# Part of a block-wise matrix product done in seven products of quarters instead of eight

## The chip, the cores and the metric

The kernel runs on one core of one Trainium2 chip. The metric is the device time of one execution in microseconds (us). The core's engines work side by side, each through its own queue in order: TensorE (PE in the rows, its weight loads PEld), VectorE (DVE), ScalarE (ACT), GpSimd (POOL) and SyncE (SP), which here issues the loads. What a matmul writes lands in PSUM; the rest lives in SBUF.

## The reference

A decoder trunk of two layers over 256 tokens of 1024 channels. Each layer has a mixer (attention in the first, a convolution module in the second) and an expert mixer with 16384 experts, and this last one takes most of the time:

```python
def peer(h, w_pq, sub_keys, expert_u, expert_v):
    ...
    def chunk(args):
        xc, ec, gc = args
        u = expert_u[ec]
        act = jax.nn.gelu(jnp.einsum('cd,chkd->chk', xc, u))
        w = gc.astype(xc.dtype) * act
        return jnp.einsum('chk,chkd->cd', w, expert_v[ec])
```

The kernel doesn't gather the 128 chosen experts of each token. It multiplies all experts: the first table gives a value for every expert and token, the gates (zero where an expert isn't chosen) are multiplied in, and the second table is multiplied with the result: out[256 tokens, 1024] = W[256, 16384] x V[16384, 1024]. The change is in this second product.

## The kernel before, in words

Everything is fp32. A product is made from parts: each operand is rounded to a high part (`hi`, written by ScalarE) and the rest is kept as a low part (`lo`, written by VectorE), and `mm3` (lines 126 to 132) does three matmuls: high by high, high by low, low by high. Each streams 512 columns.

The second table comes in 128 blocks of 128 experts, two at a time: 64 pairs in each layer (line 612). For a pair, the 512 weights per expert row (two blocks of 256 tokens) lie in the store tile `st`; ScalarE writes their high parts `wh` (line 616) and VectorE their low parts `wo` (line 617), in a ring of four pairs. Then `s2` (line 159) takes the two blocks of the table by `weights` (line 98): SP loads a block of 128x1024 into one of four `raw` buffers (line 95), ScalarE casts it to one of three `hi` buffers (line 106), VectorE subtracts to one of three `lo` buffers (line 112). The sums of the whole stage lie in four PSUM banks `acc[t][h]`, t one of two tiles of 128 tokens, h one of two halves of 512 channels. A pair is thus eight products (two blocks, two t, two h) of three matmuls: 24.

At the end of a layer's stage the four banks are added to the residual `x` (line 221) when the next norm is made. In the first layer, from the middle of the stage on, ScalarE also writes scaled diagonals for the convolution that follows (line 423), three a pair.

The order in which each engine's instructions go out is not that of the code: a planner of the language (`schedule_with_timeline_sim=True`) orders them, by the order of the code and by when it thinks operands and buffers are ready. Only where `after` or `keep_in_program_order` stands is the order given by hand.

Of the kernel before, what the change touches and what calls it, by code (L numbers as in the profile page):

```python
# [7 lines left out]
F32 = mybir.dt.float32  # L8
F32R = mybir.dt.float32r
# [3 lines left out]
ALU = mybir.AluOpType  # L13
AX = mybir.AxisListType

P = 128
D = 1024
KC = D // P
T = 256
# [13 lines left out]
NK = 128  # L33
# [4 lines left out]
HI = NK // 2  # L38
# [3 lines left out]
G0 = 24  # L42
G1 = 60
OH = 3 * NK * TB
TMP = 512 + NT * D


# [9 lines left out]
class Trunk:  # L57
# [101 lines left out]
    def s2(self, acc, src, aTs, n0, n, pool_share=0, between=None):  # L159

        if n0 + len(aTs) == n:
            pool_share = 0
        blocks = [(n0 + k, self.weights(src[n0 + k], pool_share), a) for k, a in enumerate(aTs)]
        th = [(t, h) for t in range(NT) for h in range(2)]
        if n0 + len(aTs) == n:
            order = [(b, t, h) for t, h in th for b in blocks]  # L170
        elif n0 == 0:
            order = [(b, t, h) for t in range(NT) for b in blocks for h in range(2)]
        else:
            order = [(b, t, h) for b in blocks for t, h in th]
        prev = None
        for (i, w, a), t, h in order:
            if n0 == 0 and t == 1 and between is not None:
                between()
                between = None
            mms = self.s2_mm(acc, w, a, t, h, i == 0, i == n - 1)  # L180
            if n0 + len(aTs) == n:
                if prev is not None:
                    self.after(mms[0], prev)
                prev = mms[-1]


    def setup(self):
# [59 lines left out]
    def norm_open(self, g):  # L247
        self.xT = [self.one.tile([P, KC, T], F32R, tag=k, name=self.nm(k)) for k in ("xh", "xo")]
        self.g = g
        self.tmp = self.cutter(self.work.tile([P, TMP], F32, tag="oh", name=self.nm("tmp")))  # L250
        self.junk = self.tmp(512)
# [316 lines left out]
    def peer(self, l, acc):  # L568
        nc, I = self.nc, self.I
        new = lambda: self.store_tile("st").rearrange("p (i t) -> p i t", t=T)  # L570
        st = [new()]
        sl = lambda i: st[i // HI][:, i % HI:i % HI + 2, :]

        g = self.gain(2 * l + 1, st[0][:, HI - D // T:, :].rearrange("p i t -> p (i t)"))
        xT = self.norm_T(g, acc)
        U, V = I["u"][l], I["v"][l]
        self.route_open(l)
        for h in range(PH):
            ps = self.s1_pair([I["wpq"][l, 2 * h], I["wpq"][l, 2 * h + 1]], xT, POOL_Q, h == 0)
            qT = self.qT[h % 2]  # L580
            nc.scalar.copy(qT, ps)
            self.route_scores(l, h, qT)
        route = self.route_steps()
        steps = 2 * (PH + 13)
        nb = T // TB
        half = NK // 4
        done = 0
        for pi in range(NK // 2):
            if pi == G0:
                for _ in route:  # L590
                    pass
                st.append(new())
                self.gates_open()
                self.one_hots(0)
            due = min(max(0, pi + 1 - G0) * nb // (G1 - G0), nb)
            todo = list(range(done, due))
            done = due
            ps = self.s1_pair([U[2 * pi], U[2 * pi + 1]], xT,
                              between=lambda j: [self.gate_bank(b, j, 2 * pi, st) for b in todo])
            for b in todo:  # L600
                if b + 1 < nb:
                    self.one_hots(b + 1)
            self.expert_rows(ps, sl(2 * pi), done * TB)
            if pi < G0:
                for _ in range((pi + 1) * steps // G0 - pi * steps // G0):
                    next(route, None)
        acc = self.s2_open()
        ring = 4
        wh = self.one.tile([P, ring, 2, T], F32R, tag="xh", name=self.nm("wh"))
        wo = self.one.tile([P, ring, 2, T], F32R, tag="xo", name=self.nm("wo"))  # L610
        w0 = self.work.tile([P, 2, 2, T], F32R, tag="oh", name=self.nm("w0"))
        for pi in range(NK // 2):
            w, r = sl(2 * pi), pi % ring

            h, o = (wh[:, r], wo[:, r]) if pi else (w0[:, 0], w0[:, 1])
            nc.scalar.copy(h, w)  # L616
            nc.vector.tensor_tensor(o, w, h.bitcast(F32), op=ALU.subtract)  # L617
            parts = [(h[:, j, :], o[:, j, :]) for j in range(2)]
            self.s2(acc, V, parts, 2 * pi, NK)
            if pi < half:  # L620
                pass
            elif l + 1 == DEPTH:
                if pi == half:
                    self.g_out = self.gain(2 * DEPTH, self.store_tile("g")[:, 0:D])
            else:
                if pi == half:
                    prep = self.conv_prep(l + 1)
                for _ in range(-(-(CDG + 1) // half)):
                    next(prep, None)
        return acc  # L630
# [130 lines left out]
    def gates_open(self):  # L761
        oh = self.work.tile([P, 2 * OH], F16, tag="oh", name=self.nm("oh"))
        self.oh = oh.rearrange("p (r k t n e) -> p r k t n e", r=2, k=3, t=TB // 2, e=2)
# [53 lines left out]
    def finish(self, acc):  # L817
        nc = self.nc
        tmp = self.cutter(self.work.tile([P, TMP], F32, tag="oh", name=self.nm("tmp")))
        junk = tmp(512)  # L820
# [90 lines left out]
```

## Time and profile before

| | |
|---|---|
| median of 3 runs | 1880.69 us (1880.18 to 1880.77) |
| the profiled execution's own time | 1880.45 us |
| its span, first to last instruction | 1878.5 us |
| busy: TensorE, VectorE, ScalarE | 1848.9, 1308.0, 943.4 us |
| mean granted TensorE clock | 0.996 |

The profile is of one execution. Its span is 1.95 us shorter than that execution's time, for what lies before the first and after the last instruction. A matmul's row gives its duration from start to end; as matmuls overlap, 389 ns for one of 512 columns is not what it costs in a stream, which is the distance from start to start. The stage that is changed runs from about 590 to 931 us in the first layer and from about 1527 to 1871 us in the second.

### The profile page before, as it was taken

To read this page: it belongs to the slowest core of one execution; us is meant where nothing else is said; L and a number is where in the kernel's file an instruction comes from. 1 tells how busy PE (TensorE), PEld (TensorE's weight loads), DVE (VectorE), ACT (ScalarE), POOL (GpSimd) and SP (SyncE) were. 2 spreads that over 40 slices of the span, in tenths; PEclk is the share of its full clock that TensorE was granted. 3 is DMA by queue.
4 is the path that set the end of the run, shared out by engine and by line. 5 is a ranking of instruction groups with operands and counts; after the bars stand their busy time and mean duration, and the time that the engine had idled before them with its cause. 6 is when DMAs were issued, how large, how long until landed. Compare 5 with 4: busy or idle time off the path is not lost. (4 is left out here: it accounts for less than half of the span.)

```text
span 1878.5 us, 32197 instructions
## 1 busy us (share of the span) xinstructions
PE 1848.9 (98%) x12668; PEld 1690.4 (90%) x12668; DVE 1308.0 (70%) x2501; ACT 943.4 (50%) x1429; POOL 146.3 (8%) x107
## 2 busy tenths in 40 slices
PE   8999999999999999999999899999999999999998
PEld 6979999999999888888798799999999998888886
DVE  4669984788895555555587599748888855555555
ACT  4753455554445444666463534555544444444443
POOL 1213000000000000000075430000000000000000
PEclk9999999999999999999999999999999999999999
DMA  7345555444445555555542455554444455555553
GB/s 266 139 138 177 180 186 185 158 157 158 158 158 185 194 193 206 193 198 191 180 147 68 131 180 174 190 181 152 163 158 157 158 189 192 193 206 196 190 192 133
DMA packets 91736, 326.32 MB, mean 174 GB/s; under 512 B 10176, under 2 KB 12480, under 8 KB 91584
## 3 DMA queue, kind: packets, MB, share of 16 engines
q1 hardware_dynamic: 91584, 324.26, 50.5%
q8 instruction: 99, 1.62, 0.4%
q14 instruction: 53, 0.43, 0.1%
HBM read 323.17 MB, written 1.05 MB: 173 GB/s over the span
## 5 line engine op out<-in xcount | busy, mean ns | idle before, releaser
L106 ACT CAST hi<-raw 128x1024 fp32r<-128x1024 f32 x600 | 628.7, 1049 | 635.8 <-PE ps_h L146 409.4
L112 DVE TENSOR_TENSOR lo<-raw,hi 128x1024 fp32r<-128x1024 f32 x554 | 677.3, 1223 | 330.9 <-ACT hi L106 329.9
L146 PE MATMUL ps_h<-xh,hi 128*128 128x256 f32 x2560 | 734.9, 288 | 0.0
L146 PE MATMUL ps_h<-xh,lo 128*128 128x256 f32 x2560 | 721.5, 283 | 0.0
L146 PE MATMUL ps_h<-xo,hi 128*128 128x256 f32 x2560 | 718.2, 283 | 0.0
L146 PEld LDWEIGHTS ps_h<-xh,hi 128*128 128x128 f32 x2560 | 490.4, 192 | 2.0 <-issue 1.0
L146 PEld LDWEIGHTS ps_h<-xh,lo 128*128 128x128 f32 x2560 | 490.0, 192 | 0.0
L146 PEld LDWEIGHTS ps_h<-xo,hi 128*128 128x128 f32 x2560 | 488.0, 192 | 0.2
L131 PE MATMUL acc<-lo,wh 128*128 128x512 f32 x1008 | 391.1, 389 | 0.0
L132 PE MATMUL acc<-hi,wo 128*128 128x512 f32 x1008 | 391.1, 389 | 0.0
L130 PE MATMUL acc<-hi,wh 128*128 128x512 f32 x1008 | 271.3, 389 | 0.0
L132 PEld LDWEIGHTS acc<-hi,wo 128*128 128x128 f32 x1008 | 189.2, 188 | 39.4
L130 PEld LDWEIGHTS acc<-hi,wh 128*128 128x128 f32 x1008 | 189.2, 188 | 39.3
L131 PEld LDWEIGHTS acc<-lo,wh 128*128 128x128 f32 x1008 | 189.2, 188 | 39.2
L617 DVE TENSOR_TENSOR wo<-st,wh 128x512 fp32r<-128x512 f32 x126 | 86.7, 691 | 98.8 <-ACT wh L616 98.8
L616 ACT CAST wh<-st 128x512 fp32r<-128x512 f32 x126 | 77.9, 623 | 148.8 <-PE acc L131 148.8
L112 POOL TENSOR_TENSOR lo<-raw,hi 128x1024 fp32r<-128x1024 f32 x46 | 109.6, 2390 | 136.2 <-ACT hi L106 116.7
L228 POOL TENSOR_TENSOR sums<-sums,mhalf 128x1 f32<-128x1 f32 x10 | 8.7, 872 | 1009.3 <-DVE sums L225 1009.3
L793 PE MATMUL ps_g<-oh 128*128 128x128 f16 x1024 | 81.5, 220 | 0.0
L801 DVE SCALAR_TENSOR_TENSOR st<-ps_g,st 128x256 f32<-128x256 f32 (+4 forms) x224 | 74.5, 351 | 8.5 <-PE ps_g L793 8.5
L781 DVE TENSOR_TENSOR oh<-iota,slot 128x1024 f16<-128x1024 f16 x64 | 44.3, 692 | 47.8 <-PE ps_g L793 47.8
L804 ACT ACTIVATE st<-ps_g 128x256 f32<-128x256 f32 (+19 forms) x156 | 42.2, 289 | 69.1 <-DVE st L801 69.1
(168 smaller groups left out, 1242.3 us busy)
## 6 DMA issues: line engine op xcount, KB each, us to landing
raw<-in_u_dram SPq DMA_DIRECT2D x256, 512.0 KB, 3.3
raw<-in_v_dram SPq DMA_DIRECT2D x256, 512.0 KB, 3.3
raw<-in_wpq_dram SPq DMA_DIRECT2D x32, 512.0 KB, 3.4
raw<-in_pw_dram SPq DMA_DIRECT2D x24, 512.0 KB, 3.3
raw<-in_wqk_dram SPq DMA_DIRECT2D x16, 512.0 KB, 3.4
raw<-in_wv_dram SPq DMA_DIRECT2D x8, 512.0 KB, 6.3
raw<-in_wo_dram SPq DMA_DIRECT2D x8, 512.0 KB, 3.2
att<-in_bias_dram SPq DMA_DIRECT2D x4, 512.0 KB, 8.9
```

The lines of the kernel that those rows point to most:

```text
L106: ins = [nc.scalar.copy(hi, raw)]
L112: ins.append(eng.tensor_tensor(lo, raw, hi.bitcast(F32), op=ALU.subtract))
L130: return [mm(ps, wh, xh, start=first, stop=False), mm(ps, wh, xo, start=False, stop=False), mm(ps, wo, xh, start=False, stop=last)]
L131: mm(ps, wh, xo, start=False, stop=False),
L132: mm(ps, wo, xh, start=False, stop=last)]
L146: self.nc.tensor.matmul(ps[:, j, :], w[:, c * P:(c + 1) * P], x[:, c, :], start=n == 0, stop=n == len(terms) - 1)
L616: nc.scalar.copy(h, w)
L617: nc.vector.tensor_tensor(o, w, h.bitcast(F32), op=ALU.subtract)
L781: nc.vector.tensor_tensor(g0, iota, slot(0), op=ALU.is_equal)
L793: nc.tensor.matmul(ps[:, t, :], self.oh[:, b % 2, 0, tp, :, e], self.oh[:, b % 2, 1 + k, tp, :, e], start=k == 0, stop=k == 1)
L801: nc.vector.scalar_tensor_tensor(v, ps[:, :, lo:lo + m].rearrange("p t i -> p i t"), 1.0 / GS, v, op0=ALU.mult, op1=ALU.mult)
L804: nc.scalar.activation(st[half][:, m:HI, ts], ps[:, :, lo + m:lo + HI].rearrange("p t i -> p i t"), AF.Copy, scale=1.0 / GS)
```

## The change

17 of the 64 pairs of a layer (`FAST`, three or four pairs apart) go another way, `s2_seven`. The pair's product is seen as a product of two by two quarters (weights: two token tiles by two blocks of 128x128; table: two blocks by two halves of 128x512), and Strassen's scheme in Winograd's form does it in seven products instead of eight. For that VectorE makes four sums or differences of weight quarters (three of them written over the weights of the pair before, one in place) and four of table quarters (`mix`). ScalarE and VectorE then split into high and low parts seven weight quarters at once and seven table quarters in four pieces, which take four of the ring's `hi` and `lo` buffers instead of two. Three of the seven products go straight into banks of `acc`; the other four are gathered over all 17 pairs in four more PSUM banks (`quarters`), which stand in the pools of the stages before. After pair 60, `seven_end` adds these four to `x` by one copy and eight additions. The ring of `wh` and `wo` is cut from four pairs to two, and the seven weight quarters take the room behind it.

```diff
+FAST = (3, 6, 10, 13, 17, 20, 24, 27, 30, 34, 38, 41, 45, 48, 52, 55, 59)
...
+    def s2_seven(self, acc, q, srcs, a, at, parts, first, last):
...
+        nc = self.nc
+        sub = lambda o, x, y: nc.vector.tensor_tensor(o, x, y, op=ALU.subtract)
+        s1, s2, s4, a11, a21, a12, a22 = (a[:, at + k * P:at + (k + 1) * P] for k in range(-3, 4))
+        nc.vector.tensor_tensor(s1, a21, a22, op=ALU.add)
+        sub(s2, s1, a11)
+        sub(s4, a12, s2)
+        sub(a21, a11, a21)
+        ah, ao = parts
+        seven = a[:, at - 3 * P:at + 4 * P]
+        nc.scalar.copy(ah, seven)
+        sub(ao, seven, ah.bitcast(F32))
+        A = {k: (ah[:, n * P:(n + 1) * P], ao[:, n * P:(n + 1) * P])
+             for n, k in enumerate(("s1", "s2", "s4", "11", "s3", "12", "22"))}
+        left, right = slice(0, 512), slice(512, D)
+        t1, t3, t2, t4 = (self.mix[:, k, :] for k in range(4))
+        r1, r2 = (self.load(s) for s in srcs)
+        sub(t1, r1[:, right], r1[:, left])
+        sub(t3, r2[:, right], r1[:, right])
+        sub(t2, r2[:, right], t1)
+        sub(t4, r2[:, left], t2)
+        B = {}
+        for v, names in ((r1[:, left], ("11",)), (r2, ("21", "22")),
+                         (self.mix[:, 0:2, :].rearrange("p k n -> p (k n)"), ("t1", "t3")),
+                         (self.mix[:, 2:4, :].rearrange("p k n -> p (k n)"), ("t2", "t4"))):
+            n = 512 * len(names)
+            hi, lo = (self.whl.tile([P, D], F32R, tag=k, name=self.nm(k))[:, 0:n] for k in ("hi", "lo"))
+            nc.scalar.copy(hi, v)
+            sub(lo, v, hi.bitcast(F32))
...
+        for to, x, y in ((q[1], "11", "11"), (acc[0][0], "12", "21"), (acc[0][1], "s4", "22"),
+                         (q[5], "s1", "t1"), (q[7], "s3", "t3"), (q[6], "s2", "t2"), (acc[1][0], "22", "t4")):
+            mine = any(to is v for v in q.values())
+            self.mm3(to, A[x], B[y], first and mine, last and mine)
+
+    def seven_end(self, q):
...
+        nc.scalar.copy(one, q[1])
+        add(u, q[6], one)
+        add(x(0, 0), x(0, 0), one)
+        add(x(0, 1), x(0, 1), u)
+        add(x(0, 1), q[5], x(0, 1))
+        add(u, q[7], u)
+        add(x(1, 0), x(1, 0), u)
+        add(x(1, 1), x(1, 1), u)
+        add(x(1, 1), q[5], x(1, 1))
...
-        ring = 4
...
+            if pi in FAST:
+                fast = slice(4 * T, 4 * T + 7 * P)
...
+                self.s2_seven(acc, quarters, (V[2 * pi], V[2 * pi + 1]), flat, at, (wh[:, fast], wo[:, fast]),
+                              pi == FAST[0], pi == FAST[-1])
+            else:
+                n = 2 * T
+                r = pi % 2 * n
...
+            if pi == FAST[-1] + 1:
+                self.seven_end(quarters)
```

## Rows read from the trace of the kernel before

**Rows 1.** The page: busy time of each engine and its share, and two lines of the span in 40 slices (TensorE's busy tenths and its granted clock in tenths).
```profile
PE 1848.9 (98%) x12668; PEld 1690.4 (90%) x12668; DVE 1308.0 (70%) x2501; ACT 943.4 (50%) x1429; POOL 146.3 (8%) x107
...
PE   8999999999999999999999899999999999999998
...
PEclk9999999999999999999999999999999999999999
```

**Rows 2.** The page: the chain that ended last, shares of the span by line.
```profile
PE ps_h L146 22%; PE acc L130 6%; PE acc L132 6%; PE acc L131 6%; PE ps_g L793 2%; PE ps_s L676 0%; PE ps_t L269 0%; POOLq L907 0%; POOL sums L228 0%; DVE tmp L829 0%; DVE x L221 0%; PE ps_r L754 0%; DVE tmp L261 0%; DVE sums L225 0%
```

**Rows 3.** Windows of the changed stage in both layers, and one stretch after it: length, busy us (instructions) of PE, PEld, DVE, ACT and POOL, granted clock, share of the DMA engines, GB/s.
```profile
592.00:751.00 159.00, 159.00 (x704) 131.64 (x703) 92.15 (x89) 76.40 (x88) 0.34 (x2) 1.00 0.57 196
751.00:928.00 177.00, 177.00 (x783) 146.56 (x782) 101.05 (x96) 105.56 (x167) 0.00 (x0) 1.00 0.56 194
...
1532.00:1865.00 333.00, 333.00 (x1471) 275.72 (x1470) 191.38 (x182) 159.38 (x182) 0.00 (x0) 1.00 0.56 191
...
900.00:950.00 50.00, 47.86 (x255) 40.49 (x254) 30.53 (x39) 27.64 (x39) 6.57 (x4) 1.00 0.52 177
```

**Rows 4.** Timeline of ScalarE in the second layer's stage: start us, us, engine, line, operation, out<-in, shapes, count, and in brackets the idle time before with what ended it.
```profile
1604.29 0.62 ACT L616 CAST wh<-st 128x512 fp32r<-128x512 f32 x1 [1.44 <-PE acc L131]
1604.82 1.05 ACT L106 CAST hi<-raw 128x1024 fp32r<-128x1024 f32 x1
1607.24 1.05 ACT L106 CAST hi<-raw 128x1024 fp32r<-128x1024 f32 x1 [1.37 <-PE acc L132]
1609.73 0.62 ACT L616 CAST wh<-st 128x512 fp32r<-128x512 f32 x1 [1.44 <-PE acc L131]
```

**Rows 5.** Timeline of VectorE in the same stretch.
```profile
1602.89 1.23 DVE L112 TENSOR_TENSOR lo<-raw,hi 128x1024 fp32r<-128x1024 f32 x1 [1.20 <-ACT hi L106]
1604.95 0.69 DVE L617 TENSOR_TENSOR wo<-st,wh 128x512 fp32r<-128x512 f32 x1 [0.84 <-ACT wh L616]
1605.90 1.23 DVE L112 TENSOR_TENSOR lo<-raw,hi 128x1024 fp32r<-128x1024 f32 x1 [0.26 <-ACT hi L106]
1608.33 1.23 DVE L112 TENSOR_TENSOR lo<-raw,hi 128x1024 fp32r<-128x1024 f32 x1 [1.20 <-ACT hi L106]
```

**Rows 6.** Timeline of TensorE in the same stretch: the first matmuls of one block.
```profile
1604.32 1.07 PE L130 MATMUL acc<-hi,wh 128*128 128x512 f32 x4
1605.23 0.39 PE L131 MATMUL acc<-lo,wh 128*128 128x512 f32 x1
1605.45 0.39 PE L132 MATMUL acc<-hi,wo 128*128 128x512 f32 x1
1605.68 0.39 PE L131 MATMUL acc<-lo,wh 128*128 128x512 f32 x1
1605.91 0.39 PE L132 MATMUL acc<-hi,wo 128*128 128x512 f32 x1
```

**Rows 7.** Groups of instructions by line and shape, whole span: busy us, mean ns of one, idle before.
```profile
L106 ACT CAST hi<-raw 128x1024 fp32r<-128x1024 f32 x600 | 628.7, 1049 | 635.8 <-PE ps_h L146 409.4 <-PE acc L132 205.4 <-issue 11.5
L112 DVE TENSOR_TENSOR lo<-raw,hi 128x1024 fp32r<-128x1024 f32 x554 | 677.3, 1223 | 330.9 <-ACT hi L106 329.9
L617 DVE TENSOR_TENSOR wo<-st,wh 128x512 fp32r<-128x512 f32 x126 | 86.7, 691 | 98.8 <-ACT wh L616 98.8
L616 ACT CAST wh<-st 128x512 fp32r<-128x512 f32 x126 | 77.9, 623 | 148.8 <-PE acc L131 148.8
L221 DVE TENSOR_TENSOR x<-acc,x 128x512 f32<-128x512 f32 x16 | 10.8, 688 | 5.5 <-PE acc L132 5.5
L359 DVE TENSOR_TENSOR att<-s_ps,att 128x128 f32<-128x128 f32 x16 | 4.6, 286 | 17.9 <-PE s_ps L356 17.9
L131 PEld LDWEIGHTS acc<-lo,wh 128*128 128x128 f32 x1008 | 189.2, 188 | 39.2
```

**Rows 8.** Timeline of VectorE: a low part and the operation behind it, the start of the first layer's stage, and in the attention stage a reciprocal with the scalings that need it.
```profile
561.92 1.22 DVE L112 TENSOR_TENSOR lo<-raw,hi 128x1024 fp32r<-128x1024 f32 x1
563.06 0.68 DVE L617 TENSOR_TENSOR w<-st,w 128x512 fp32r<-128x512 f32 x1
...
588.22 1.23 DVE L112 TENSOR_TENSOR lo<-raw,hi 128x1024 fp32r<-128x1024 f32 x1 [1.65 <-ACT hi L106]
...
589.97 2.49 DVE L617 TENSOR_TENSOR wo<-st,wh 128x512 fp32r<-128x512 f32 x4
...
66.49 0.15 DVE L367 RECIPROCAL att<-att 128x2 f32<-128x2 f32 x1
66.67 0.55 DVE L369 TENSOR_SCALAR att<-att 128x128 f32<-128x128 f32 x2
```

**Rows 9.** Timeline of ScalarE at the start of the first layer's stage: four casts of weights in a row.
```profile
588.61 2.16 ACT L616 CAST wh<-st 128x512 fp32r<-128x512 f32 x4
```

**Rows 10.** Timeline of ScalarE in the second half of the first layer's stage: the convolution's diagonals between the casts.
```profile
802.17 1.05 ACT L106 CAST hi<-raw 128x1024 fp32r<-128x1024 f32 x1 [1.38 <-PE acc L132]
803.12 0.99 ACT L423 ACTIVATE conv<-ident,conv 128x128 f32<-128x128 f32 x3
804.66 0.62 ACT L616 CAST wh<-st 128x512 fp32r<-128x512 f32 x1 [0.55 <-PE acc L131]
```

**Rows 11.** The instructions on the tile `raw` in 1600 to 1840 us: time from a load's issue to its landing.
```profile
DMA to landing us min/median/max: 3.0/3.3/4.8
```

**Rows 12.** Timeline of TensorE: the second pair of the first layer's stage, its first block.
```profile
592.53 1.07 PE L130 MATMUL acc<-hi,wh 128*128 128x512 f32 x4
593.43 1.07 PE L131 MATMUL acc<-lo,wh 128*128 128x512 f32 x4
594.34 1.07 PE L132 MATMUL acc<-hi,wo 128*128 128x512 f32 x4
```

**Rows 13.** Timeline of VectorE at the end of the second layer's stage: the last low part and the first sums of x with the four banks.
```profile
1864.01 1.23 DVE L112 TENSOR_TENSOR lo<-raw,hi 128x1024 fp32r<-128x1024 f32 x1 [1.50 <-ACT hi L106]
1867.00 0.69 DVE L221 TENSOR_TENSOR x<-acc,x 128x512 f32<-128x512 f32 x1 [1.77 <-PE acc L132]
1868.36 0.69 DVE L221 TENSOR_TENSOR x<-acc,x 128x512 f32<-128x512 f32 x1 [0.67 <-PE acc L132]
```

More of the change, by code (lines that the diff above doesn't have):

```diff
@@ L184, in s2 @@
                 prev = mms[-1]
+    def s2_seven(self, acc, q, srcs, a, at, parts, first, last):
[27 more added lines that the diff above has]
+            sub(lo, v, hi.bitcast(F32))
+            for k, name in enumerate(names):
+                ks = slice(512 * k, 512 * k + 512)
+                B[name] = hi[:, ks], lo[:, ks]
+        for to, x, y in ((q[1], "11", "11"), (acc[0][0], "12", "21"), (acc[0][1], "s4", "22"),
+                         (q[5], "s1", "t1"), (q[7], "s3", "t3"), (q[6], "s2", "t2"), (acc[1][0], "22", "t4")):
+            mine = any(to is v for v in q.values())
+            self.mm3(to, A[x], B[y], first and mine, last and mine)
@@ new lines, in seven_end @@
+    def seven_end(self, q):
+        nc = self.nc
+        x = lambda t, h: self.x[:, t, h * 512:(h + 1) * 512]
+        one, u = self.mix[:, 0, :], self.mix[:, 1, :]
+        add = lambda o, v, w: nc.vector.tensor_tensor(o, v, w, op=ALU.add)
+        nc.scalar.copy(one, q[1])
[7 more added lines that the diff above has]
+        add(x(1, 1), q[5], x(1, 1))
@@ L607, in peer @@
         acc = self.s2_open()
-        ring = 4
-        wh = self.one.tile([P, ring, 2, T], F32R, tag="xh", name=self.nm("wh"))
-        wo = self.one.tile([P, ring, 2, T], F32R, tag="xo", name=self.nm("wo"))
-        w0 = self.work.tile([P, 2, 2, T], F32R, tag="oh", name=self.nm("w0"))
+        wh, wo = (self.one.tile([P, KC * T], F32R, tag=k, name=self.nm(k)) for k in ("xh", "xo"))
+        w0 = self.work.tile([P, 2, 2 * T], F32R, tag="oh", name=self.nm("w0"))
         for pi in range(NK // 2):
[L613 to L619, printed above, removed]
+            flat = st[2 * pi // HI].rearrange("p i t -> p (i t)")
+            at = 2 * pi % HI * T
+            if pi in FAST:
+                fast = slice(4 * T, 4 * T + 7 * P)
+                if pi == FAST[0]:
+                    self.mix = self.work.tile([P, 4, 512], F32, tag="oh", name=self.nm("mix"))
+                    quarters = {k: pool.tile([P, 512], F32, tag=tag, name=self.nm("q"))
+                                for k, pool, tag in ((1, self.ps_m, "ps_m"), (5, self.ps_m, "ps_m"),
+                                                     (7, self.ps_h, "ps_h"), (6, self.ps_h, "ps_h"))}
+                self.s2_seven(acc, quarters, (V[2 * pi], V[2 * pi + 1]), flat, at, (wh[:, fast], wo[:, fast]),
[3 more added lines that the diff above has]
+                r = pi % 2 * n
+                h, o = (wh[:, r:r + n], wo[:, r:r + n]) if pi else (w0[:, 0], w0[:, 1])
+                nc.scalar.copy(h, flat[:, at:at + n])
+                nc.vector.tensor_tensor(o, flat[:, at:at + n], h.bitcast(F32), op=ALU.subtract)
+                parts = [(h[:, j * T:(j + 1) * T], o[:, j * T:(j + 1) * T]) for j in range(2)]
+                self.s2(acc, V, parts, 2 * pi, NK)
+            if pi == FAST[-1] + 1:
+                self.seven_end(quarters)
             if pi < half:
```

## The prediction

> **What bounds the kernel now.** I read the page's busy shares and its PE and clock slices first [rows 1], then the chain that ended last [rows 2]. TensorE is busy 98% of the span, in nearly every slice, at a granted clock of 9 tenths or more, and the chain is matmul groups from end to end; the change touches lines 130 to 132, each 6% of it. Then the windows of the stage that is changed, one per layer [rows 3]: in 592 to 928 us and in 1532 to 1865 us TensorE has no idle time, VectorE is busy 58% and ScalarE 48% (60% where it also writes the convolution's diagonals), the DMA engines 56%. So in this stage time is matmuls, and anything taken off TensorE is time saved as long as VectorE and ScalarE still deliver each block's two parts before TensorE wants them.
>
> The timelines give the period and the lead. ScalarE's cast of a pair's weights comes every 5.44 us [rows 4], so one pair of blocks is 24 matmuls in 5.44 us: 226.7 ns each, 0.68 us for a product of three. VectorE works three times in that period [rows 5] and sits idle between: 0.84, 0.26 and 1.20 us before the three operations. Its waits are all for casts, and the casts wait for TensorE to give a buffer back. So VectorE and ScalarE are held by the ring of three hi/lo buffers, not by their own speed. The lead: TensorE begins a pair at 1604.32 [rows 6], and the last low part of that pair ended at 1602.89 + 1.23 = 1604.12 [rows 5]. VectorE is thus one whole pair minus half a block ahead, which is all that the ring allows.
>
> **What the change removes.** In 17 of 64 pairs in each of two layers, one product of eight goes: 34 x 3 matmuls = 102, at 226.7 ns = **-23.1 us**. All of them lie on the path, by the windows. Their weight loads go with them (188 ns against the 226.7 ns period, hidden before and after).
>
> **What it adds, on VectorE.** Durations first [rows 7]: 128x1024 in 1.22 us, 128x512 in 0.69 us (the same from PSUM), 128x128 in 0.29 us. Operations that don't need one another start before the one ahead has ended: four of 512 take 2.49 us, so 0.60 us from start to start, and a low part of 1024 is followed after 1.14 us [rows 8]. One that needs the result ahead of it starts 0.03 us after its end (the reciprocal and the scaling behind it, 66.49 + 0.15 to 66.67). A changed pair then costs:
> - sums of the weights: s1, s2, s4 hang on one another, 3 x 0.31, and the fourth 0.20: 1.1 us
> - low part of seven slices, 896 columns: 0.69 + 384 x (1.22 - 0.69)/512 = 1.09 us, by start to start 1.0
> - four differences of 512: 2 to 4 hang on one another in part: 2.5 us
> - low parts: one of 512 and three of 1024: 0.60 + 3 x 1.14 = 4.0 us
>
> Together 8.65 us, where an ordinary pair costs 0.60 + 2 x 1.14 = 2.9. TensorE needs 21 x 0.2267 = 4.76 us for the changed pair. Taken alone VectorE is short by 3.9 us, so the balance must be made over a group, a changed pair and the two or three ordinary ones up to the next (eight gaps of three and eight of four): three pairs are 14.4 us of VectorE against 15.6 of TensorE, four 17.3 against 21.1. It fits, at 92% and 82%.
>
> **On ScalarE.** 512 columns 0.62 us, 1024 1.05 us, 896 interpolated 0.94 us [rows 7]; start to start 0.51 for 512 [rows 9], 0.95 for 1024 likewise. A changed pair: 0.85 + 0.51 + 3 x 0.95 = 4.2 us, ordinary 2.4; a group of three 9.0 of 15.6 us, and with three diagonals a pair, 0.99 us [rows 10], 12. Cover is ample; what can hurt is only what stands ahead of what in its queue.
>
> **Loads.** As many, of the same size; SP issues them in the same order. A slot of the four raw buffers is now held until the differences are done. A load lands in 3.3 us [rows 11] and goes out when the low part four blocks ahead is done, some 11 us before use: nothing.
>
> **Does the lead cover a changed pair?** Clock zero: TensorE begins the ordinary pair k-1. VectorE has finished that pair's low parts (-0.2). Good order: the sums and their low part were done in the pair before, whose idle time (5.44 - 2.9 = 2.5 us) holds them (1.1 + 1.0); the weights of pair k-1, whose place three of the sums take, are split by then, as they are cast two pairs ahead. Then the differences run 0 to 2.5; low part of the first quarter to 3.1; buffer of block (k-1, first) comes back at 2.72, cast, low part to 5.0; TensorE begins k at 5.44, does three products to 7.48; buffer of (k-1, second) came back at 5.44, cast by 6.5, or 7.0 behind the cast of the next weights, low part by 7.7 or 8.2; meanwhile TensorE has the four matmuls that want only casts, to 8.4; the last low part is done by 9.3, when it is wanted. TensorE ends at 10.2 = 5.44 + 4.76. **Lower bound 0** a pair. After one ordinary pair the old lead is back (TensorE begins k+2 at 15.6, its last low part, whose buffer comes back at 12.9, is done by 15.2), so the lag doesn't add up from one changed pair to the next.
>
> Bad order: VectorE takes the sums only at zero, waits for ScalarE's cast of the seven slices (0.94 us), then low part, then differences, as written: first quarter at 6.2, second at 7.4, third 8.5, fourth 9.7. TensorE then ends at 10.7, or 11.3 if it too goes strictly as written: **0.5 to 1.1 us** a pair.
>
> Which? The issue order is made by the scheduler, and the trace shows its way. TensorE does all four hi x wh matmuls of a block first and then alternates [rows 6], although the code has three in turn; in the first pair after the start it does four, four, four [rows 12], just when the weights' low part was later than the block's (VectorE did wo at 589.97 after lo at 588.22 [rows 8]); the weights' cast takes the slot of the pair that just ended, of four, so it is for four pairs on, while the block's cast behind it is for two pairs on [rows 4]. So work goes out when it is ready, and the sums and differences will be drawn into the idle 2.5 us before. I am near the lower bound, yet seven products on three buffers leave 0 to 0.5 us of margin, and each queue has one or two heads that can be late: **0.2 us** a pair, 34 x 0.2 = **+6.8 us**.
>
> A rule to weigh: start to start shows 0.60 us where one operation lasts 0.69 [rows 8]. The Trainium skill, VectorE: DVE Perf Modes, section The DRAIN you can't avoid, has the next operation start only when the pipe of the one before is empty (it goes on to except those that nothing holds). By it no overlap could be counted: rival 4 below gives the time. The rows disagree wherever operations don't hang on one another.
>
> **The ends.** After pair 60 the four extra banks are folded into x: one copy and eight additions of 128x512 at 0.60 to 0.69 us [rows 7], some 5.1 us on VectorE, in line before the low parts of pair 61. The first of these would end near 7.0 us after pair 60 began, wanted at 5.44 + 0.9: 0.6 us late. Bounds 0 and 1.2 a layer; I take 0.5: **+1.0 us**. Hidden otherwise by the idle time of pairs 61 to 63 (7.5 us), and done before the sums of x that follow the last matmul [rows 13]. Ring of weights cut from four to two: a cast at the end of pair k-2 for pair k has 5.44 us for 0.62 + 0.69: nothing. The stage's start: two weight parts less ahead, the sums of pair 3 instead: nothing.
>
> **Sum.** -23.1 + 6.8 + 1.0 = -15.3 us against the profiled execution's own 1880.45 us (span 1878.5, 1.95 around it; the median of the runs, 1880.69, is 0.24 above): **1865.2 us**.
>
> **The rivals.**
> 1. No stall: 0 and 0 from the lower bounds: -23.1, 1857.4 us. For it: the walk above ends on time. Against: no margin at the third and fourth low part.
> 2. Half the gain stays: 0.35 to 0.6 us a pair, -11 to -2 us with the ends, 1869 to 1878. For it: the queue of ScalarE, where the cast of the seven slices can stand behind a cast that waits for a buffer.
> 3. **Slower**: VectorE and ScalarE issue a changed pair as written, so each one costs 0.95 us, the wait for the cast of seven slices. 34 x 0.95 = 32.3 + 1 - 23.1 = +10.2: 1890.7 us. It decides from 0.65 us a pair ((23.1 - 1.0)/34). For it: VectorE has only 1.2 us to spare in a group of three. Against: the order in [rows 4, 6, 12].
> 4. VectorE can't overlap: full durations give 4 x 0.32 + 1.09 + 4 x 0.69 + 0.69 + 3 x 1.22 = 9.5 and 3.1 us, 15.7 of 15.6 in a group of three. The seven operations before the third low part come 0.6 us later, of which some 0.3 shows: 0.5 us a pair, -23.1 + 17 + 1 = -5, 1875 us. This one stands with the page named above.
> 5. The products go but the matmuls slow down, since more banks are written in turn: 226.7 ns holds for the pairs now, with four banks in turn; I see no reason. To take the gain back every one of the 2 x 1485 matmuls of the stage would have to be 8 ns slower.
>
> A clock loss is not among them: 2.1 us idle in 900 to 950 left the granted clock at 1.00 (2.4 GHz) there [rows 3].
>
> **Chances.** Forecast's case (0.05 to 0.35 us a pair, 1859 to 1870) 0.55; rival 1 0.14; rivals 2 and 4 up to 1876.9 together 0.12; within 0.2% (3.8 us, about what a measurement of this kernel can tell from no change), 1876.9 to 1884.5, 0.07; rival 3 0.11; rival 5 0.01. Faster 0.81, same 0.07, slower 0.12. The range is 1857.4 to 1876: both unknown costs at their lower bounds, and rivals 2 and 4 in; left out is 0.2.
>
> **What would show it.** 102 matmuls fewer at 227 ns; VectorE's differences standing in the idle time of the pair before; TensorE idle in the two windows together about 7 us, in pieces under 0.3 us at each changed pair, named for VectorE's low parts. VectorE 34 x 5.8 = 196 us busier by start to start. Wrong if: idle pieces of 0.7 us or more with VectorE waiting for the cast of the seven slices (rival 3), VectorE without idle time through groups of three (rival 4), or matmuls off 227 ns (rival 5).

## The result and the profile after

The changed kernel takes 1868.88 us (median of 4 runs, 1866.46 to 1871.39), the kernel before 1880.43 beside it: a ratio of 0.9939, 95% interval 0.9922 to 0.9956. That is 11.5 us faster where the sum forecast 15.3. The profiled execution took 1868.77 us, its span is 1866.8. The four times spread over 5 us, the four of before over 1.0; on the chips of the runs below those of before spread over 1.9 to 3.7.

The page of the kernel after, in the lines that answer [rows 1]: 102 matmuls fewer, VectorE 176.6 us busier, the clock as before.
```profile
PE 1836.3 (98%) x12566; PEld 1667.5 (89%) x12566; DVE 1484.6 (80%) x2857; ACT 1006.1 (54%) x1499; POOL 146.2 (8%) x107
...
PEclk9999999999999999999999999999999999999999
```
The windows of the changed stage in both layers, after (columns as in [rows 3]): the granted clock is 1.00 (2.4 GHz) as before, VectorE has gone from 58% to 84%, and TensorE has short stops where it had none.
```profile
575.00:915.00 340.00, 338.92 (x1517) 275.36 (x1516) 284.55 (x366) 218.80 (x298) 0.34 (x2) 1.00 0.60 197
1515.00:1852.00 337.00, 336.24 (x1478) 273.77 (x1477) 286.75 (x368) 198.50 (x226) 0.00 (x0) 1.00 0.60 195
```
A busy TensorE hides short stops, since a row goes on to the end of its last matmul. So I measure the stage itself, from the start of its first matmul to the start of its last. TensorE's timeline before, both layers:
```profile
587.06 0.40 PE L130 MATMUL acc<-hi,w 128*128 128x512 f32 x1
...
935.02 0.39 PE L132 MATMUL acc<-hi,wo 128*128 128x512 f32 x1
...
1522.69 0.40 PE L130 MATMUL acc<-hi,w 128*128 128x512 f32 x1
...
1870.65 0.39 PE L132 MATMUL acc<-hi,wo 128*128 128x512 f32 x1
```
And after:
```profile
586.62 0.40 PE L132 MATMUL acc<-hi,w 128*128 128x512 f32 x1
...
929.98 0.39 PE L134 MATMUL acc<-hi,xo 128*128 128x512 f32 x1
...
1517.68 0.40 PE L132 MATMUL acc<-hi,w 128*128 128x512 f32 x1
...
1859.02 0.39 PE L134 MATMUL acc<-hi,xo 128*128 128x512 f32 x1
```
Before, both stages last 347.96 us; 51 matmuls at 226.7 ns less would be 336.40. After they last 343.36 and 341.34: 6.96 and 4.94 us, 11.9 in all, are lost in stops, 0.35 us a changed pair. -23.12 + 11.90, and a stage that begins 0.44 us earlier, give -11.66, the difference of the spans (1878.5 to 1866.8).

The stops are of two kinds. **Regular**: 0.16 to 0.17 us at nearly every changed pair. ScalarE and TensorE at a changed pair that begins at 1645.70, after:
```profile
1645.67 0.62 ACT L690 CAST xh<-st 128x512 fp32r<-128x512 f32 x1 [1.39 <-PE acc L133]
1646.19 2.00 ACT L222 CAST hi<-mix 128x1024 fp32r<-128x1024 f32 x2
```
```profile
1647.74 1.01 PE L132 MATMUL q<-hi,xh 128*128 128x512 f32 x3
1648.58 0.40 PE L132 MATMUL acc<-hi,xh 128*128 128x512 f32 x1
```
ScalarE casts the next pair's weights (0.52 us from start to start) ahead of the last two table pieces. TensorE has done three products by 1647.74 and takes the four high-by-high matmuls on these two pieces. The third of them wants the last piece, whose cast ends at 1648.19, and its weight load (188 ns, [rows 7]) waits with it. Three matmuls in a row take 0.39 + 2 x 0.227 = 0.85 us, these 1.01. Of these 0.16 us the late start of the third is 0.06 (1648.25 for 1648.19); the rest follows it, since the fourth starts only 0.33 us later.

**Irregular**: up to 0.8 us, at some pairs. The worst of them, after: SyncE, ScalarE, VectorE, then TensorE nine us later.
```profile
814.07 0.33 SPq L97 DMA_DIRECT2D raw<-in_v_dram  x1
```
```profile
816.62 1.05 ACT L108 CAST hi<-raw 128x1024 fp32r<-128x1024 f32 x1
```
```profile
816.75 0.69 DVE L691 TENSOR_TENSOR xo<-st,xh 128x512 fp32r<-128x512 f32 x1 [0.84 <-ACT xh L690]
820.04 0.69 DVE L197 TENSOR_TENSOR mix<-raw 128x512 f32<-128x512 f32 x1 [2.61 <-DMA raw<-in_v_dram]
...
820.86 1.22 DVE L114 TENSOR_TENSOR lo<-raw,hi 128x1024 fp32r<-128x1024 f32 x1
```
```profile
829.22 0.50 PE L133 MATMUL acc<-lo,xh 128*128 128x512 f32 x1 [0.61 <-DVE lo L197]
...
831.56 0.50 PE L133 MATMUL q<-lo,xh 128*128 128x512 f32 x1 [0.24 <-DVE lo L197]
```
The first difference t1 stands at VectorE's head from 817.4 and waits 2.61 us for its load, issued at 814.07 and landed 6.0 us later. Behind it stands a low part whose cast was done at 817.67. VectorE is then late by that much, and the next changed pair's low parts reach TensorE late. Over the stage of the first layer, 575 to 915 us, the waits are (engine, tile, line; us in total, times, longest):
```profile
DVE mix L197 <- DMA raw<-in_v_dram: 14.4, 14, 2.6
...
PEld q L133 <- DVE lo L197: 4.6, 13, 0.7
PEld q L132 <- ACT hi L222: 4.4, 14, 0.3
```
The tile `raw` in 1600 to 1840 us, after, against [rows 11]: loads land in 4.1 us, not 3.3.
```profile
DMA to landing us min/median/max: 3.1/4.1/5.7
```
The waits come with this longer landing. In the two stages 29 differences wait for a load, 27.3 us in all. Each of them stood ready 3.4 us or more after the issue of its load, and these loads took 4.2 to 6.0 us; at the 3.3 us of [rows 11] none would have waited. Before, most loads are issued 2.4 to 3.0 us apart; after, a quarter of them within 1.6 us of the one ahead. The late load above is the third of four issued within 4.7 us (811.26 to 815.93), which landed after 3.2, 4.7, 6.0 and 5.3 us. No run spaced the loads alone, so that the bunching delays them is not shown.

### The profile page after: what moved, and what is told of

Same layout as the page of the kernel before. It is cut to its first block, busy times and chain, and to the rows that moved or that the text cites. A ratio compares the mean times of both kernels' runs of the same rounds, so it can differ in the third digit from the quotient of the medians.

```text
span 1866.8 us, 32407 instructions
## 1 busy us (share of the span) xinstructions
PE 1836.3 (98%) x12566; PEld 1667.5 (89%) x12566; DVE 1484.6 (80%) x2857; ACT 1006.1 (54%) x1499; POOL 146.2 (8%) x107
## 5 line engine op out<-in xcount | busy, mean ns | idle before, releaser
L108 ACT CAST hi<-raw 128x1024 fp32r<-128x1024 f32 x532 | 557.0, 1049 | 540.6 <-PE ps_h L148 409.3
L114 DVE TENSOR_TENSOR lo<-raw,hi 128x1024 fp32r<-128x1024 f32 x486 | 592.5, 1221 | 172.3 <-ACT hi L108 170.5
L133 PE MATMUL acc<-lo,xh 128*128 128x512 f32 x870 | 338.8, 391 | 1.2 <-DVE lo L197 1.1
L134 PE MATMUL acc<-hi,xo 128*128 128x512 f32 x870 | 337.9, 390 | 0.0
L132 PE MATMUL acc<-hi,xh 128*128 128x512 f32 x870 | 248.8, 391 | 0.0
L133 PEld LDWEIGHTS acc<-lo,xh 128*128 128x128 f32 x870 | 163.5, 188 | 38.2 <-DVE lo L197 2.7
L132 PEld LDWEIGHTS acc<-hi,xh 128*128 128x128 f32 x870 | 163.5, 188 | 34.3 <-ACT hi L108 0.5
L134 PEld LDWEIGHTS acc<-hi,xo 128*128 128x128 f32 x870 | 163.7, 188 | 33.8
L114 POOL TENSOR_TENSOR lo<-raw,hi 128x1024 fp32r<-128x1024 f32 x46 | 109.5, 2387 | 136.3 <-ACT hi L108 117.3
L691 DVE TENSOR_TENSOR xo<-st,xh 128x512 fp32r<-128x512 f32 x92 | 63.1, 688 | 27.6 <-ACT xh L690 27.5
L197 DVE TENSOR_TENSOR lo<-mix,hi 128x1024 fp32r<-128x1024 f32 x68 | 80.2, 1221 | 5.4 <-ACT hi L222 5.4
```

The source lines that it names most:

```text
L108: ins = [nc.scalar.copy(hi, raw)]
L114: ins.append(eng.tensor_tensor(lo, raw, hi.bitcast(F32), op=ALU.subtract))
L132: return [mm(ps, wh, xh, start=first, stop=False), mm(ps, wh, xo, start=False, stop=False), mm(ps, wo, xh, start=False, stop=last)]
L133: mm(ps, wh, xo, start=False, stop=False),
L134: mm(ps, wo, xh, start=False, stop=last)]
L197: sub = lambda o, x, y: nc.vector.tensor_tensor(o, x, y, op=ALU.subtract)
```

## Experiments

The theory (A) says that the two losses are made by the order in VectorE's and ScalarE's queues, the regular one by the next weights' cast, the irregular one by differences that stand ahead of low parts and wait for late loads. The rival (B) says that VectorE has too little time, and any order loses as much. A ratio is always to runs of the kernel before on the same chip, with its 95% interval.

**1. The change again.** No edit.

> The changed kernel as it is, for its spread beside the next three. Both theories: near 1868.9 us, single executions from 1866 to 1872 us, where the kernel before stays within 1 us.

1871.24 us (1869.51 to 1872.7), 0.9941 (0.9928 to 0.9955). It is the measure for runs 2 to 4, on the same chip. The kernel before spreads over 2.7 us there (1880.46 to 1883.18), not within the 1 that was expected. In the profiled execution, the slowest, the two stages take 344.28 and 341.79 us: 13.3 us lost.

**2. The next weights' cast behind the changed pair's last cast.**
```diff
-            nc.scalar.copy(hi, v)
+            self.hi_seven = nc.scalar.copy(hi, v)
...
-                nc.scalar.copy(h, flat[:, at:at + n])
+                cast = nc.scalar.copy(h, flat[:, at:at + n])
+                if pi - 1 in FAST:
+                    self.after(cast, self.hi_seven)
```


> Theory A (order of the queues): in the trace of the change TensorE stands 0.16 to 0.17 us at each changed pair before the first matmul on the last cast (t2, t4), since ScalarE casts the next pair's weights (0.52 us) ahead of the two table casts. Here that cast goes behind them, nothing else changes. The 34 stops go: -5.8 us, near 1863 us. Theory B (VectorE has too little time in groups of three, whatever the order): its work is the same, so the stop moves to the low parts and the time stays at 1868 to 1869 us.

1865.62 us (1863.9 to 1870.52), 0.9913 (0.9900 to 0.9927): 5.6 us under run 1. ScalarE's timeline has the order turned round:
```profile
1647.85 2.19 ACT L222 CAST hi<-mix 128x1024 fp32r<-128x1024 f32 x2 [1.62 <-PE acc L134]
1649.94 0.61 ACT L690 CAST xh<-st 128x512 fp32r<-128x512 f32 x1
```
The three matmuls that took 1.01 us, on TensorE:
```profile
1649.69 0.90 PE L132 MATMUL q<-hi,xh 128*128 128x512 f32 x3
```
Three in a row take 0.85 us, so 0.05 is left. The waits in the first layer's stage:
```profile
PEld acc L133 <- DVE lo L114: 3.7, 8, 0.9
...
PEld q L132 <- ACT hi L222: 0.8, 4, 0.2
```
The waits for the last piece's cast go from 4.4 to 0.8 us, and a part comes back at the next ordinary pair's low parts (L114). The waits of differences for loads stay (16.9 us in the second layer's stage, 3.5 the longest), and the spread is 6.6 us. By the medians the move is worth 5.6 us. The profiled execution, again the slowest, shows less: its stages take 342.91 and 340.21 us, so 10.3 us are lost instead of run 1's 13.3.

**3. The first difference behind the first low part of the pair before.**
```diff
+        self.lows = getattr(self, "lows", [])[-1:] + [ins[-1]]
...
-        sub(t1, r1[:, right], r1[:, left])
+        self.after(sub(t1, r1[:, right], r1[:, left]), self.lows[0])
```


> Theory A: where the gap is four pairs, the first table difference stands in VectorE's queue ahead of both low parts of the pair before, and waits there up to 2.6 us for its load. Here it is queued behind the first of these low parts; the work is the same. VectorE's waits for loads at that place (27 us in all) shrink or cost less, TensorE's stops of 0.4 to 0.8 us go: -2 to -4 us, 1865 to 1867 us, and the executions lie closer together. Theory B: same work, same time, 1868 to 1869 us.

1867.12 us (1866.99 to 1867.83), 0.9921 (0.9908 to 0.9935): 4.1 us under run 1, and the spread falls from 3.2 to 0.8 us. The waits in the first layer's stage, against those of the change above:
```profile
PEld q L133 <- ACT hi L223: 5.6, 17, 0.5
DVE mix L198 <- DMA raw<-in_v_dram: 5.0, 14, 0.7
```
VectorE waits 5.0 us instead of 14.4, and the regular wait is there at all 17 pairs. Low parts are still named at seven places, but for 1.5 us in all and 0.2 at most; in the second layer at none. The stages take 340.59 and 340.06 us: 7.9 us are lost, 13.3 in run 1. That the late loads also made the spread is not shown, since the kernel before spreads over 2.7 us on this chip and run 5, which has no difference, over 2.95.

**4. Both orders.** The edits of 2 and 3.

> Both changes of order together. Theory A: the two gains add, -8 to -10 us, 1859 to 1861 us, near the 1857.4 us of no stall at all. Theory B: 1868 to 1869 us.

1865.91 us (1864.87 to 1866.42), 0.9913 (0.9898 to 0.9928): 5.3 us under run 1, not 8 to 10. The stages take 340.98 and 338.95 us, so 0.21 us a changed pair is still lost. One reason shows on VectorE, and below it on TensorE, in the first layer's second half:
```profile
791.20 2.36 DVE L198 TENSOR_TENSOR lo<-mix,hi 128x1024 fp32r<-128x1024 f32 x2 [0.85 <-ACT hi L223]
793.73 0.69 DVE L694 TENSOR_TENSOR xo<-st,xh 128x512 fp32r<-128x512 f32 x1 [0.17 <-ACT xh L691]
794.68 2.36 DVE L114 TENSOR_TENSOR lo<-raw,hi 128x1024 fp32r<-128x1024 f32 x2 [0.26 <-ACT hi L108]
```
```profile
794.76 1.15 PE L133 MATMUL acc<-hi,xh 128*128 128x512 f32 x4
795.97 0.50 PE L134 MATMUL acc<-lo,xh 128*128 128x512 f32 x1
```
The next, ordinary pair's weights and blocks are now cast later, and its first low part ends at 794.68 + 1.22 = 795.90. TensorE, which began that pair at 794.76, wants it after four matmuls, at 795.67, and starts at 795.97. What was taken from one piece is given back at the next. Here ScalarE also writes three diagonals in between (0.98 us); in the second layer, without them, the stage loses 2.55 us, in the first 4.58.

**5. The matmuls alone.** The changed pairs are prepared as ordinary ones.
```diff
-        nc.vector.tensor_tensor(s1, a21, a22, op=ALU.add)
...
-        sub(t4, r2[:, left], t2)
+        four = a[:, at:at + 4 * P]
+        nc.scalar.copy(ah, four)
+        sub(ao, four, ah.bitcast(F32))
+        for s, names in zip(srcs, (("11", "21", "t1", "t3"), ("22", "t2", "t4"))):
+            hi, lo = self.weights(s)
```


> The 34 changed pairs are prepared as ordinary pairs are (one cast and one low part of four weight slices, two hi/lo buffers of 1024), without the eight sums and differences; the 21 matmuls into the same eight banks and the end with its additions stay. The products then multiply the wrong quarters: left out is what makes the scheme a matrix product. Both theories say that the 102 matmuls are worth their full 23.1 us when nothing else changes: 23.1 us under the kernel before, 1859 where that one takes 1882. If time is lost already here (more banks in turn, the end of the stage), it is that much higher, and the stall of 0.35 us a pair must be read smaller.

1859.7 us, 0.9887 (0.9872 to 0.9902). TensorE's timeline, first layer, first and last matmul of the stage:
```profile
588.12 0.40 PE L132 MATMUL acc<-hi,w 128*128 128x512 f32 x1
...
924.52 0.39 PE L134 MATMUL acc<-hi,xo 128*128 128x512 f32 x1
```
336.40 us, and 336.40 in the second layer: 51 x 226.7 ns to the hundredth, with eight banks in turn and the end's nine operations in place. The median is only 21.2 us under before. This execution reached the first stage at 588.12, not 587.06, and took 0.9 us longer between the stages, where the kernels are alike. What differs there is the granted clock. Right behind the stage TensorE stands idle for 1.44, 0.41 and 0.27 us in both; then it had 1.2 GHz here from 928.0 to 931.4 us, and 2.4 GHz in the profile of before, which shows in the same eight transposes, before and in this run:
```profile
938.84 1.32 PE L269 MATMUL ps_t<-ident,tmp 128*128 128x128 f32 x8 [0.27 <-DVE tmp L261]
```
```profile
928.34 1.97 PE L314 MATMUL ps_t<-ident,tmp 128*128 128x128 f32 x8 [0.27 <-DVE tmp L306]
```
It was 1.2 GHz for 3.4 us at 129 us too, before the first stage. Two executions of one kernel can thus differ by a microsecond or two outside the stages; the stages' own lengths, at 2.4 GHz in every profile but that of run 11, don't have this in them.

**6. Without the changed pairs' loads.** Their table quarters are read from columns of the store tile.
```diff
-        r1, r2 = (self.load(s) for s in srcs)
+        far = 8192 if at < 8192 else 0
+        r1, r2 = (a[:, far + k * D:far + (k + 1) * D] for k in range(2))
```


> The 68 loads of the changed pairs are left out, and their table quarters are read from columns of the store tile, so their sums, differences, casts and products work on other numbers, in the same count and shape. Theory A (order of queues: the irregular stops come from differences that wait for a load at VectorE's head): VectorE's waits on the mix tile go, the irregular stops with them, the regular 0.17 us a pair stays: 5 to 6 us under the change. Theory B (VectorE has too little time): the same work on VectorE, so the same stalls: within 2 us of the change.

1888.44 us, 1.0039 (1.0025 to 1.0053): slower than before, and neither theory's number. The planner, with nothing to wait for, issued the next changed pair's differences far earlier. VectorE, then TensorE, right behind a changed pair:
```profile
1664.91 1.29 DVE L197 TENSOR_TENSOR mix<-st 128x512 f32<-128x512 f32 x2
1666.11 1.22 DVE L114 TENSOR_TENSOR lo<-raw,hi 128x1024 fp32r<-128x1024 f32 x1
```
```profile
1667.39 0.50 PE L133 MATMUL acc<-lo,xh 128*128 128x512 f32 x1 [0.30 <-DVE lo L114]
```
Two differences, not needed for two pairs yet, stand ahead of a low part that TensorE wants at once. The same work, without a single late load, costs some 18 us more than the change (1.0039 for 0.9941): order alone does that (run 9 reads the same columns without the loss). But as a test of the loads it is spoilt, so run 9 repeats it in the change's order.

**7. The order of the code.** VectorE and ScalarE keep it within a changed pair.
```diff
+        keep = self.tc.keep_in_program_order
+        sub = lambda o, x, y: keep(nc.vector.tensor_tensor(o, x, y, op=ALU.subtract))
...
-            nc.scalar.copy(hi, v)
+            keep(nc.scalar.copy(hi, v))
```


> The sums, differences, casts and low parts of a changed pair keep the order in which the code has them, on VectorE and on ScalarE. Rival 3 of the prediction, worked out for that order: 0.95 us a changed pair, 34 x 0.95 + 1 - 23.1 = 10.2 us over the kernel before, 1892 where that one takes 1882, with a stop at each changed pair while VectorE waits for the cast of the seven slices. If the waits for that cast are hidden by the lead whatever the order, it stays near the change, 1871.

1885.03 us (10 runs), 1.0023 (1.0013 to 1.0032). This is slower than before, as rival 3 has it, but by less: both stages take 349.44 us, 13.04 over 336.40, so 0.77 us a changed pair, not 0.95. VectorE waits for the cast of the seven slices, but less than its 0.94 us, since the ordinary weights' low part, 0.60 us, comes in between:
```profile
1652.48 1.09 DVE L200 TENSOR_TENSOR xo<-st,xh 128x896 fp32r<-128x896 f32 x1 [0.41 <-ACT xh L207]
```
That is one part of the 0.77 us. TensorE's own waits in the second layer's stage are named for casts of table pieces (10.3 us, 17 times) and for low parts (9.7 us, 34 times); how the loss divides was not taken apart.

**8. Every second pair.**
```diff
-FAST = (3, 6, 10, 13, 17, 20, 24, 27, 30, 34, 38, 41, 45, 48, 52, 55, 59)
+FAST = tuple(range(3, 60, 2))
```


> 29 changed pairs a layer instead of 17 (every second pair from the fourth to the sixtieth), else the change as it is. 174 matmuls fewer than before, 39.4 us. By VectorE's own time: a changed and an ordinary pair are 11.0 us by its busy time (2.9 + 176.6/34 more, + 2.9) to 11.5 by the prediction's start to start, against 10.2 of TensorE and 10.9 for the two in the kernel before: VectorE is the bound, 58 x 0.1 to 0.7 us, 7 to 36 us over the kernel before, with no idle time on VectorE in the stage. If VectorE's time were no limit and each changed pair cost the same 0.35 us as with 17: 58 x (0.68 - 0.35) = 19 us under it.

1925.95 us, 1.0244 (1.0230 to 1.0258): 45 us over before, more than the 7 to 36 expected. VectorE's timeline, one period:
```profile
1640.95 0.69 DVE L197 TENSOR_TENSOR mix<-raw 128x512 f32<-128x512 f32 x1
1641.56 0.69 DVE L197 TENSOR_TENSOR mix<-raw,raw 128x512 f32<-128x512 f32 x1
...
1649.16 0.69 DVE L691 TENSOR_TENSOR xo<-st,xh 128x512 fp32r<-128x512 f32 x1 [0.49 <-ACT xh L690]
...
1652.79 0.69 DVE L197 TENSOR_TENSOR mix<-raw 128x512 f32<-128x512 f32 x1
```
A changed and an ordinary pair come every 11.84 us, with 0.49 us idle: 11.35 us of VectorE, where the prediction's prices give 8.65 + 2.9 = 11.55. Here theory B holds: VectorE is the bound, busy for 348.87 of the 367 us from 1549 to 1916. In a group of three it needs one ordinary pair more, 11.35 + 2.9 = 14.25 us, and TensorE gives it 15.6.

**9. Without the loads, in the change's order.** The edit of 6, with each difference held at its place in the change by `after`.
```diff
...
+        self.after(d2, d3)
+        if pi > FAST[0]:
+            self.after(d1, self.wo_last if far else self.lows[1])
+            self.after(d3, self.lows[1 if far else 2])
...
```


> As the run without the changed pairs' loads (their table quarters are read from columns of the store tile, on other numbers), but each difference, the cast and the low part of the first quarter are held at the places in the queues that they have in the change; only some 128x128 sums stand elsewhere within the same pair. That run was slower because its differences, ready at once, stood ahead of the low parts of the pair behind the changed one. If the irregular stops of the change are waits for late loads at VectorE's head, they go and the regular 0.17 us stay: 1859.7 (matmuls alone) + 34 x 0.17 = 1865.5, 5 to 6 us under the change (ratio to before 0.991). If they come from the differences' place ahead of the low parts, whenever the loads land: 1869 to 1873, as the change (0.994).

1866.45 us (1865.44 to 1866.98), 0.9920 (0.9907 to 0.9934), where A said 1865.5 and the change has 0.9939 and 0.9941: some 4 us less than the change. The stages take 340.66 and 339.95 us, 7.8 us lost instead of 11.9. The first layer's waits of the matmuls for casts:
```profile
PEld q L133 <- ACT hi L229: 5.6, 17, 0.5
```
The regular stop is left at 17 of 17 pairs. Of waits for low parts seven are left in the first layer, 0.2 us at most, and none in the second: the same as in run 3. Differences at the same place cost nothing when their loads are there. So the irregular loss is that of late loads.

**10. The differences on GpSimd.**
```diff
-        sub(t1, r1[:, right], r1[:, left])
...
+        nc.gpsimd.tensor_tensor(t1, r1[:, right], r1[:, left], op=ALU.subtract)
```


> The four table differences of a changed pair go to GpSimd, idle in this stage; its 128x1024 subtraction takes 2.39 us in the profile after, so some 1.2 us for 512 and 4.8 us a pair. VectorE has 2.5 us less a changed pair and waits for no load. Theory A: the irregular stops go, the regular ones (ScalarE's casts) stay: 1865 to 1867 (0.991 to 0.992). Theory B: with a quarter of VectorE's added work gone, both go: 1860 (0.989). Against both: the chain of differences is twice as long, or GpSimd and VectorE slow each other when they read SBUF together (1.22 us for a low part grows): at the change or above it, 1871 and more.

1884.91 us (11 runs), 1.0020 (1.0011 to 1.0029): above the change, the last of the three cases expected. GpSimd, then VectorE, at one changed pair:
```profile
1648.99 1.49 POOL L212 TENSOR_TENSOR mix<-raw 128x512 f32<-128x512 f32 x1 [13.07 <-DMA raw<-in_v_dram]
...
1651.94 1.35 POOL L214 TENSOR_TENSOR mix<-raw,mix 128x512 f32<-128x512 f32 x1
1653.37 2.16 POOL L215 TENSOR_TENSOR mix<-raw,mix 128x512 f32<-128x512 f32 x1
```
```profile
1649.24 2.89 DVE L197 TENSOR_TENSOR st<-st 128x128 f32<-128x128 f32 x3
1652.05 2.32 DVE L114 TENSOR_TENSOR lo<-raw,hi 128x1024 fp32r<-128x1024 f32 x1
1654.29 2.18 DVE L197 TENSOR_TENSOR xo<-st,xh 128x896 fp32r<-128x896 f32 x1
```
The three sums take 2.89 us instead of 0.69, the low part 2.32 instead of 1.22, the seven slices 2.18 instead of 1.09. The low part ends at 1654.37, one low part after the GpSimd operation that ended at 1653.29: in these rows the engines take turns, and what leaves VectorE's queue comes back as waiting.

**11. The differences on GpSimd, every second pair.** The edits of 8 and 10.

> The differences on GpSimd and 29 changed pairs a layer. 174 matmuls fewer, 39.4 us. VectorE: 11.5 - 2.5 = 9.0 us of the 10.2 that TensorE needs for a changed and an ordinary pair, GpSimd 4.8. If it fits and only the regular 0.17 us a pair is lost: 58 x (0.68 - 0.17) = 30 us under before, 1851. If each changed pair costs 0.35 us as in the change: 19 us under, 1862. If GpSimd's differences stand in the way of the casts or slow VectorE by a tenth (9.0 to 9.9): no gain over the change, 1871 and more.

2059.04 us, 1.0938 (1.0918 to 1.0957): 178 us over before. Of the three expectations only the last had the side right, and none the size.

**12. Every third pair, both orders.** The edits of 2 and 3, and 19 changed pairs a layer.
```diff
+FAST = tuple(range(3, 60, 3))
```


> The two reorderings together (next weights' cast behind the changed pair's last cast, first difference behind the first low part of the pair before) with 19 changed pairs a layer, all three pairs apart. 114 matmuls fewer, 25.8 us. By the prediction's price VectorE needs 14.4 us of the 15.6 of a group of three, so no group is left in which VectorE has 3.8 us to spare. If that slack isn't needed and the 0.21 us a changed pair of the run with both orders stays: 25.8 - 38 x 0.21 = 17.8, some 2 us under that run, 0.9905 of before. If the groups of four are what lets VectorE catch up: stops that grow from pair to pair, 0.35 us and more a pair, 1868 or above (0.993).

1862.34 us (1862.04 to 1862.79), 0.9904 (0.9888 to 0.9921): 18.0 us under before, and below the change's interval. The stages take 339.02 and 337.61 us against 347.96 - 57 x 0.2267 = 335.04: 0.17 us a changed pair. The slack of the groups of four is not needed. From runs 2 and 4 its interval does not set it apart.

## Why the prediction was right, and where its terms were off

**Removed, -23.1 us: right**, to the hundredth in both stages of run 5. Rival 5 (slower matmuls) is out with it.

**VectorE, 8.65 us a changed pair: right** within 0.2 us (11.35 for 11.55 in run 8); its busy time grew by 176.6 us for the 196 forecast. Rival 4 is out: operations start 0.61 us apart though each lasts 0.69, in run 8 too, where VectorE is the bound and a changed and an ordinary pair take 11.35 us of it, not the 12.6 of full durations (9.5 + 3.1). Run 12, all in groups of three, loses 0.17 us a pair and not 0.5. The sentence of the Trainium skill, VectorE: DVE Perf Modes, section The DRAIN you can't avoid, is thus not what sets the pace of these operations; the rows fit the exception that the page makes, of an operation that nothing holds.

**The lead walk, 0.2 us a changed pair: mis-sized.** It measured 0.35 (11.9 us for 6.8), of which 0.17 is the regular stop and 4 to 5 us in all are the late loads of the next paragraph; the 1 to 2 us that are left were not taken apart. The 0.2 was a margin for late heads of queues that the walk did not name, and it was worked out from neither stop, so that the sum comes within 4 us of the result is in part luck. The lower bound of 0 was wrong by a step that can be named: the walk timed the cast of the third piece ("by 6.5, or 7.0 behind the cast of the next weights") and then let TensorE do "the four matmuls that want only casts". Two of the four want the fourth piece, which the walk gave no cast of its own. In the trace that cast ends 2.49 us after TensorE began the pair (1645.70 to 1648.19, 7.93 on the walk's clock), when its matmul should already start, and 0.17 us a pair goes there: 5.8 us in all. Run 2 moved one cast and took 5.6 us off by the medians, 3.0 by the profiled stages.

**"Loads: nothing": wrong**, some 4 to 5 us (runs 3 and 9). The 11 us of lead are those of a low part. The prediction itself drew the differences into the pair before, and a difference reads the same block: t1 stood ready to go 3.4 us after its load was issued (814.07 to 817.4). That still leaves room for the 3.3 us which the prediction took from the kernel before. What it had wrong is that this time would stay: it rose to 4.1 us in the median, and to 4.2 to 6.0 for the loads that a difference waited for.

**The ends, 0.5 us a layer: 0.** Run 5 holds all nine operations and loses nothing. Nor does the change itself: from the start of pair 60 (908.44) to the last matmul (929.98) it takes 21.54 us, the kernel before 21.53 (913.49 to 935.02).

**What would show it.** 102 matmuls fewer and differences in the idle time of the pair before: as said. Idle TensorE, "7 us in pieces under 0.3 us, named for VectorE's low parts": half so. The regular pieces are named for ScalarE's casts, the irregular ones for low parts, and these reach 0.8 us.

**Rival 3, slower as written: right in sign** (run 7), 0.77 us a pair for 0.95, and above the 0.65 from which it decides. The prediction's argument against it, that the planner sends work out when it is ready, held; run 6 shows that the same habit can cost more than the code's own order. **Rivals 1 and 2:** the time lies at the edge between the forecast's case and rival 2, whose named mechanism (ScalarE's cast of the seven slices behind a cast that waits) isn't the one seen.

**Theories A and B.** A is borne out for both losses by runs 2, 3 and 9; B begins to hold between groups of three (run 12) and of two (run 8). What A didn't foresee is that the gains don't add up (run 4). That the remaining 0.2 us a pair is in good part the next ordinary pair's low parts was read from its trace, and no run took it away. Nor did a run try why loads land later.

## What to carry to other kernels

Walk a lead to the last piece that a stage wants, not to the first that looks tight, and give every cast and load of a moved step a due time of its own. A step drawn ahead into idle time takes its inputs' due times along, and in an in-order queue whatever stands behind it inherits its wait. A landing time read from the kernel before need not hold once a change issues the loads at other moments. Before moving work to an idle engine, look in the trace for both engines at work side by side on the same kind of operands.

## What was unexpected of the hardware

VectorE's subtractions, which read two tiles, and GpSimd's hold each other up: with both at work, 1.22 us became 2.32 and 1.35 became 2.16 (run 10). The Trainium skill, SBUF — State Buffer, section SBUF: two separate sides, has the two share a pair of ports that one operation holds for its whole length when VectorE has two inputs in SBUF and GpSimd reads SBUF too; the rows of run 10 agree (GpSimd ends at 1653.29, VectorE's low part 1.08 us later).

A matmul that waited for its part is followed by the next after 0.33 to 0.34 us, not 0.23 (829.22 and 829.56 for one, 1648.25 and 1648.58 for another, in the change). Each of these stops thus costs some 0.11 us more than the late start, and in the regular stop this is two thirds of the loss.

In run 11 TensorE's granted clock fell in the stage itself. The first time, TensorE had stood idle for 2.08 us up to 612.04; then it had 1.2 GHz instead of 2.4 until 615.6 us:
```profile
612.04 0.71 PE L133 MATMUL acc<-lo,xh 128*128 128x512 f32 x1 [2.08 <-DVE lo L114]
```
```profile
612.20:615.50 3.30, 3.30 (x8) 2.57 (x9) 3.30 (x3) 0.00 (x0) 0.92 (x1) 0.50 0.61 178
```
The mean from 575 to 915 us was 0.94. In every other profile the stage kept 1.00, with all its stops.
